# A four-mixer decoder layer on one core: the mixers' rank against the dense products, and finer tracing

## The chip, the core and the metric

The kernel runs on one core of a Trainium2 chip. The metric is the device time of one execution in microseconds.

## What is computed

One layer of a hybrid recurrent decoder, for 512 prompt positions and 8 sequences of 8 sample positions (576 columns in all), in float32. The input is normalised, one projection feeds four token mixers (ssd: Mamba-2; s5: a diagonal state space; hg: HGRN2; rw: RWKV-7), their outputs are gated, merged and projected back, and a gated MLP with a short convolution follows. Cut to the core:

```python
proj = rmsnorm(x, norm1_w) @ w_in
y_ssd, y_s5, y_hg, y_rw = ssd_mixer(...), s5_mixer(...), hgrn_mixer(...), rwkv_mixer(...)
gates = sigmoid(xn @ w_merge + b_merge)
merged = (gates[0] * (y_ssd @ w_br_ssd) + gates[1] * (y_s5 @ w_br_s5)
          + gates[2] * (y_hg @ w_br_hg) + gates[3] * (y_rw @ w_br_rw))
x = x + merged @ w_out
up = causal_dwconv(rmsnorm(x, norm2_w) @ ffn_up)
x = x + (gelu(up_gate) * up_val) @ ffn_down
```

The mixers' new states are outputs too.

## The kernel before

**Dense products.** Activations lie transposed, 128 features by 576 columns, each split into a high and a low part. A weight tile is loaded by SP (`weights`, L182), cast to its high part on ACT (L169) and subtracted to its low part on DVE or POOL (L170). `dense` (L211) makes an output tile of 128 x 576 in two halves of 288 columns; `part` (L219) issues three products per 128 inputs: high by high (L223), high by low (L224), low by high (L225), names `dn`. A dense tile of eight inputs is thus 48 products. The evacuation of a half and all of a weight tile's instructions have rank HIGH.

**Mixers.** Each is a generator that issues a piece of its work and yields a number, the piece's cost. Their products are small, their results are named `mxrw`, `mxs`, `mxhg` and `mxssd`. rw runs as stream "a", s5, hg and ssd one behind the other as stream "b". The last steps of rw (from L1795) write the sample states out: products (L1797), transposes (L94), a copy on ACT (L1806) into one buffer, tB, and two stores; then `finish` normalises each of two heads' groups in two column pieces (L1835 to L1849): head sums on PE (L1423, L1424), a square (L1838), a reciprocal root on DVE (L176 to L180), three steps on POOL up to L1848. These use tB too.

**Order of the work.** The order on the engines has two stages. First `drive` (L2288) traces three streams: "a", "b" and `dense_stream` (L2199). It always continues the stream with the lowest clock, and adds to that clock what the generator yields; for a mixer, times a factor of SLOW (L29). Then a scheduler lays the traced instructions out on each engine: of those that it holds ready it takes the one of lowest rank. An instruction's rank is its number in the trace less an offset, and a mixer's offset is HIGH, a million: a ready mixer instruction goes ahead of every dense product. On the chip each engine then takes its instructions in that order.

**Dense stream.** `dense_stream` traces the projections u, rw, hg, dt, xbc and z (55 tiles). Then it computes gate tiles ahead (`gate`, L427) and stores them to memory (`spill`), up to 32, as long as the mixers are not done. When stream "a" is done ("a" in `done`), the pools `late`, `gp` and `yp` are opened in the place of rw's, the S5 outputs are loaded (yg, L446; `load_split`) and turned into the GLU's input yh, and there follow the GLU (L2181), the branches rw, s5, hg, ssd (`branch`, L473) and the tail: w_out and the MLP. A gate that was not stored is computed within its branch.

Of the kernel before, what the change touches and what calls it, by code (L numbers as in the profile page):

```python
# [25 lines left out]
GELU = 0.7978845608028654  # L26
HIGH = 1000000

SLOW = {"rw": 4.65, "s5": 1.62, "hg": 2.88, "ssd": 1.86}  # L29


STRASSEN = (1, 0, 1, 0, 0, 0, 1, 0, 0, 0, 1)
# [8 lines left out]
class Kern:  # L41
# [169 lines left out]
    def dense(self, w, k0, kt, c0, mt, xh, xl, evac, inner=None):  # L211

        for m in range(mt):
            wt = self.weights(w, k0, kt, c0 + m * P, inner)
            for j in range(2):
                self.part(wt, slice(j * H2, (j + 1) * H2), xh, xl, m, evac)
            yield m

    def part(self, wt, sl, xh, xl, m, evac):  # L219
        nc = self.nc  # L220
# [181 lines left out]
def project(K, name, c0, order):  # L402

    nc, tc = K.nc, K.tc
    for m in order:
        st = K.stage.tile([P, T], F32, tag="st", name=K.n("st"))

        def evac(_, sl, ps, st=st):
            if name == "u":

                nc.scalar.copy(out=st.rearrange("p (s c) -> p s c", s=LS)[:, :, sl.start // LS:sl.stop // LS],
                               in_=ps.rearrange("p (c s) -> p s c", s=LS))
            else:
                nc.scalar.copy(out=st[:, sl], in_=ps)

        for _ in K.dense(K.I["w_in"][0], 0, 8, c0 + m * P, 1, K.xh, K.xl, evac, 16 if name == "u" else None):
            d = K.dram.tile([LS, P, T // LS] if name == "u" else [P, T], F32, name=f"pd_{name}{m}")
            with tc.high_priority(offset=HIGH):
                if name == "u":
                    nc.sync.dma_start(out=d.rearrange("s p c -> p s c"), in_=st.rearrange("p (s c) -> p s c", s=LS))  # L420
                else:
                    nc.sync.dma_start(out=d, in_=st)
            K.proj[(name, m)] = d
            yield 6000


def gate(K, b, m, g):  # L427

    nc = K.nc

    def evac(_, sl, ps):
        nc.scalar.activation(g[:, sl], ps, AF.Tanh, bias=K.vc("b_merge", b * 8 + m), scale=0.5)  # L432

    for _ in K.dense(K.I["w_merge"][0], 0, 8, b * D + m * P, 1, K.xh, K.xl, evac):
        yield 6000


def load_split(K, y, scale=None, turn=False, keep=None):
# [34 lines left out]
def branch(K, b, wname, ys, cols=None, done=None):  # L473

    nc, tc = K.nc, K.tc
    yh, yl = [h for h, _ in ys], [l for _, l in ys]
    kt = len(ys)
    for m in range(8):
        g = K.gp.tile([P, T], F32, tag="g", name=K.n("g"))
        if (b, m) in K.gates:  # L480
            nc.sync.dma_start(out=g, in_=K.gates[(b, m)])
        else:
            yield from gate(K, b, m, g)
        first = not K.started[m]
        K.started[m] = True

        def evac(_, sl, ps):
            o = K.merged[m] if first else g
            nc.vector.scalar_tensor_tensor(out=o[:, sl], in0=g[:, sl], scalar=1.0, in1=ps, op0=ALU.add, op1=ALU.mult)  # L489

        for _ in K.dense(K.I[wname][0], 0, kt, m * P, 1, yh, yl, evac):
            if cols is not None:
                nc.gpsimd.tensor_tensor(out=g, in0=g, in1=cols, op=ALU.mult)
            if not first:
                nc.gpsimd.tensor_tensor(out=K.merged[m], in0=K.merged[m], in1=g, op=ALU.add)
            if done:
                done(m)
            yield 750 * kt


def conv_state_out(K, cs, ktaps, nt, prompt, sample, pool):
# [65 lines left out]
def tail(K):  # L567
# [27 lines left out]
    with K.mc:  # L595
# [48 lines left out]
            nc.vector.tensor_tensor(out=x1[m][:, sl], in0=ps, in1=res[m][:, sl], op=ALU.add)  # L644

        for m in K.dense(I["w_out"][0], 0, 8, 0, 8, mh, ml, evac):
            with tc.high_priority(offset=HIGH):
                sides(m)
            if m == 0:
                nc.scalar.activation(acc, x1[m], AF.Square)  # L650
            else:
                sq = K.stage.tile([P, T], F32, tag="st", name=K.n("sq"))
                nc.scalar.activation(sq, x1[m], AF.Square)
                (nc.vector if m == 7 else nc.gpsimd).tensor_tensor(out=acc, in0=acc, in1=sq, op=ALU.add)
# [106 lines left out]

    K.spare["t"] += ["c", "w", "w"]
    for m in K.dense(down, k0, n, 0, LAST, ah, al, evac):
        if m:
            turn(m - 1)
        if m == 1:
            states_out()
# [54 lines left out]
def hgrn(K, ctx):  # L822
# [41 lines left out]
    def head(h):  # L864
# [108 lines left out]
        for c in range(4):  # L973
            cs = slice(c * P, (c + 1) * P)
            nc.tensor.matmul(po[:, cs], vt[:, c, :], att[:, cs], start=True, stop=c == 0)
            if c:
                nc.tensor.matmul(po[:, cs], S[:, c - 1, :], qR[:, cs], start=False, stop=True)
        nc.scalar.copy(out=o[:, :TP], in_=po)
        pso = K.ps()
        S0 = wk("S0", (P, NS, P), 1)  # L980
        nc.sync.dma_start(out=S0, in_=I["state_hgrn"][0, :, h].rearrange("b k v -> k b v"))
        nc.tensor.matmul(pso[:, :64], svt, satt, start=True, stop=False)
        for b in range(NS):
            nc.tensor.matmul(pso[:, b * LS:(b + 1) * LS], S0[:, b, :], qR[:, TP + b * LS:TP + (b + 1) * LS],
                             start=False, stop=b == NS - 1)
        nc.scalar.copy(out=o[:, TP:], in_=pso[:, :64])
        yield 3500
        nc.gpsimd.tensor_tensor(out=S0, in0=S0, in1=stot[:, 64:72].unsqueeze(2).to_broadcast([P, NS, P]), op=ALU.mult)
        for j in range(2):
            bs = slice(j * 4, j * 4 + 4)  # L990
            vm = wk("kt", (P, 4, P))[:64]
            nc.gpsimd.tensor_tensor(out=vm, in0=svt.unsqueeze(1).to_broadcast([64, 4, P]),
                                    in1=sm[:64, bs].unsqueeze(2).to_broadcast([64, 4, P]), op=ALU.mult)
            pt = K.ps()
            nc.tensor.matmul(pt, skt, vm.rearrange("p b v -> p (b v)"), start=True, stop=True)
            sv = S0[:, bs, :].rearrange("p b v -> p (b v)")
            nc.vector.tensor_tensor(out=sv, in0=sv, in1=pt, op=ALU.add)
        nc.sync.dma_start(out=O["s_hgrn"][0, :, h].rearrange("b k v -> k b v"), in_=S0)
        yield 3000

        sq, rn = f, kL
        nc.scalar.activation(sq, o, AF.Square)
# [53 lines left out]
def s5(K, ctx):  # L1056
# [142 lines left out]
    for qt in range(4):  # L1199
# [41 lines left out]
        for a in range(GP):  # L1241
            for ri, cb in ((0, cbr), (1, cbi)):
                nc.tensor.matmul(pk[:, a * 32:(a + 1) * 32], W[ri][:, a].rearrange("p s j -> p (s j)"), cb[:, a, :],
                                 start=ri == 0, stop=ri == 1)
        yield 4000

        Kc = wp.tile([P, 8, 16], F32, tag="Kc", name=K.n("Kc"))
        TT(out=Kc, in0=pk[:, :P].rearrange("p (g j) -> p g j", j=16), in1=dsk[:, qt * 8:(qt + 1) * 8, :], op=ALU.add)
# [13 lines left out]
        for ri in range(2):  # L1262
# [3 lines left out]
                    es = slice(g2 * 64, g2 * 64 + 64)  # L1266
                    nc.tensor.matmul(pt[es, b * NCK:(b + 1) * NCK], Mz[:, b, ri, es], U[:, 2 * b + g2, :], start=True, stop=True)
            nc.scalar.copy(out=Z[:, ri].rearrange("p g c -> p (g c)"), in_=pt[:, :GP * NCK])
        yield 2500

        E = Z[:, :, :, :NPC].rearrange("p r g (c k) -> p r g c k", k=8)
        a8r, a8i = Pr[:, 8, gs], Pi[:, 8, gs]
# [40 lines left out]
        for g2 in range(2):  # L1313
            es = slice(g2 * 64, g2 * 64 + 64)
            pt = K.ps()
            for a in range(GP):
                gq = 2 * a + g2
                o = pt[:, a * NCK:(a + 1) * NCK]
                nc.tensor.matmul(o, Mt[:, gq].rearrange("p t j -> p (t j)"), U[:, gq, :], start=True, stop=False)
                for ri in range(2):  # L1320
                    nc.tensor.matmul(o, Mc[ri][es, a].rearrange("p t j -> p (t j)"), H[es, ri, a, :], start=False, stop=ri == 1)
            nc.scalar.copy(out=Y.rearrange("p (a g) c -> p g a c", g=2)[:, g2], in_=pt[:, :4 * NCK].rearrange("p (a c) -> p a c", a=GP))
            yield 2000
        d = K.dram.tile([P, T], F32, name=f"y_s5{qt}")
        dv = d.rearrange("(g j) (t c) -> t j g c", j=16, c=NCK)
        for t in range(8):
# [529 lines left out]
def ssd(K, ctx):  # L1856
# [135 lines left out]
    for hf in range(2):  # L1992
# [10 lines left out]
        for c in (4, 0, 1, 2, 3):  # L2003
# [74 lines left out]
            if samp:  # L2078
# [6 lines left out]
                for q in range(2):  # L2085
# [6 lines left out]
                    for b in range(0, NS, 4):  # L2092
                        pt = K.ps()
                        for b2 in range(4):
                            K.turn(pt[:, b2 * P:(b2 + 1) * P], h0[:, b + b2].rearrange("p g n -> p (g n)"))
                        nc.scalar.copy(out=h0T[b // 4], in_=pt.rearrange("p (b q) -> p b q", b=4))
                    po = K.ps()[:, :P]
                    for b in range(NS):
                        nc.tensor.matmul(po[:, b * 16:(b + 1) * 16], h0T[b // 4][:, b % 4, :], CS[:, b].rearrange("p g t -> p (g t)"), start=True, stop=True)
                    od = wk("Gm", (P, P), 2)  # L2100
                    TT(out=od.rearrange("p (g b t) -> p g b t", g=2, t=LS), in0=po.rearrange("p (b g t) -> p g b t", g=2, t=LS),
                       in1=eB.rearrange("p (g q) (b t) -> p q g b t", g=2, t=LS)[:, q], op=ALU.mult)
# [3 lines left out]
                    for g in range(2):  # L2106
# [3 lines left out]
                                         start=True, stop=True)  # L2110
                        TT(out=h0[:, :, g, :], in0=h0[:, :, g, :], in1=pn.rearrange("p (b n) -> p b n", b=NS), op=ALU.add)
                        nc.sync.dma_start(out=view(O["s_ssd"][0], g), in_=h0[:, :, g, :])
                    yield 3500
            elif c:
                po = K.ps()
                for q in range(2):
# [64 lines left out]
def glu(K, ys, yt):  # L2181
# [3 lines left out]
    for m in range(4):  # L2185
# [3 lines left out]
            nc.scalar.activation(g[:, sl], ps, AF.Tanh, bias=K.vc("s5_glu_b", m), scale=0.5)  # L2189

        for _ in K.dense(K.I["s5_glu_w"][0], 0, 4, m * P, 1, yh, yl, evac):
            nc.vector.scalar_tensor_tensor(out=g, in0=g, scalar=1.0, in1=yt[:, m], op0=ALU.add, op1=ALU.mult)
            d = K.dram.tile([P, T], F32, name=f"y_s5g{m}")
            nc.sync.dma_start(out=d, in_=g)
            K.y_s5g.append(d)
            yield 3000


def dense_stream(K):  # L2199
# [88 lines left out]
def drive(K, streams):  # L2288

    live = [[0, i, g, nm] for i, (g, nm) in enumerate(streams)]  # L2290
    while live:
        s = min(live, key=lambda v: v[:2])
        try:
            if s[3]:
                K.stream, K.label = s[3], K.now.get(s[3], "")
                with K.tc.high_priority(offset=HIGH):
                    s[0] += SLOW[K.now.get(s[3], "rw")] * max(next(s[2]), 1)
            else:
                s[0] += max(next(s[2]), 1)
# [47 lines left out]
```

## Time and profile before

| | us |
|---|---|
| median of 3 runs | 1699.29 |
| runs | 1692.22, 1699.29, 1717.2 |
| the profiled execution | 1718.78 |
| its span, first to last instruction | 1717.1 |
| PE busy in the span | 1629.7 |
| DVE, POOL, ACT busy | 1186.2, 789.6, 696.0 |

The profile is one execution. PE is the engine of matrix products, DVE, ACT and POOL work elementwise, SP issues the DMAs. A busy time is the union of the shown durations of an engine's instructions; products overlap, so the distance from start to start says more than a duration. The granted clock has two levels, 1.0 (2.4 GHz) and 0.5 (1.2 GHz); a value between is a mean over a stretch.

### The profile page before, as it was taken

How to read it: one execution, taken by the hardware profiler on the slowest of the kernel's cores; microseconds unless marked ns; L12 is line 12 of the kernel's file. 1: busy time of each engine (PE TensorE's matmuls, PEld its weight loads, DVE VectorE, ACT ScalarE, POOL GpSimd, SP SyncE). 2: the span in 40 equal slices, each digit the busy share in tenths (PEclk: the TensorE clock that was granted, in tenths of full speed). 3: DMA queues.
4: the chain of work that ended last, by engine and by line, in shares of the span. 5: the costliest groups of instructions: out<-in, count | busy, mean ns of one | idle time of the engine just before them, and what ended most of it. 6: DMA issues, size and time to landing. Idle time of an engine off the chain costs nothing. (4 is left out here: it accounts for less than half of the span.)

```text
span 1717.1 us, 32744 instructions
## 1 busy us (share of the span) xinstructions
PE 1629.7 (95%) x12164; PEld 1473.1 (86%) x12164; DVE 1186.2 (69%) x2584; ACT 696.0 (41%) x1489; POOL 789.6 (46%) x1013
## 2 busy tenths in 40 slices
PE   6989999999999999999998999998998999999997
PEld 4888888888798898778887988888998999989897
DVE  7888886986684388333347664695479975985985
ACT  6333232433343344222245353332356643653653
POOL 5645342534322464121244563375676734743750
PEclk7999888998899999879999999999999999999999
DMA  7555553642462455231345553665422332232332
GB/s 202 141 129 138 139 119 84 174 120 77 142 182 75 122 168 163 63 99 59 100 145 155 152 161 100 203 193 156 124 90 75 99 99 74 75 99 74 87 105 71
DMA packets 356453, 207.62 MB, mean 121 GB/s; under 512 B 110884, under 2 KB 328358, under 8 KB 356294
## 3 DMA queue, kind: packets, MB, share of 16 engines
q1 hardware_dynamic: 356293, 205.53, 42.6%
q8 instruction: 96, 1.57, 0.4%
q14 instruction: 64, 0.52, 0.1%
HBM read 151.54 MB, written 53.02 MB: 119 GB/s over the span
## 5 line engine op out<-in xcount | busy, mean ns | idle before, releaser
L223 PE MATMUL dn<-xh,whi 128*128 128x288 f32 x1392 | 430.1, 309 | 6.4 <-ACT gst L432 2.7
L224 PE MATMUL dn<-xl,whi 128*128 128x288 f32 x1392 | 431.8, 310 | 1.9 <-DVE xl L170 1.6
L225 PE MATMUL dn<-xh,wlo 128*128 128x288 f32 x1392 | 428.5, 308 | 0.0
L223 PEld LDWEIGHTS dn<-xh,whi 128*128 128x128 f32 x1392 | 271.4, 195 | 22.4 <-issue 9.1
L224 PEld LDWEIGHTS dn<-xl,whi 128*128 128x128 f32 x1392 | 271.8, 195 | 15.8 <-issue 8.5
L225 PEld LDWEIGHTS dn<-xh,wlo 128*128 128x128 f32 x1392 | 271.6, 195 | 10.7 <-issue 7.0
L169 ACT CAST whi<-wraw 128x512 fp32r<-128x512 f32 (+1 forms) x278 | 173.4, 628 | 236.4 <-PE dn L224 225.9
L170 POOL TENSOR_TENSOR wlo<-wraw,whi 128x512 fp32r<-128x512 f32 x92 | 131.4, 1429 | 195.2 <-ACT whi L169 171.1
L170 DVE TENSOR_TENSOR wlo<-wraw,whi 128x512 fp32r<-128x512 f32 (+1 forms) x186 | 150.5, 810 | 81.2 <-ACT whi L169 68.5
L262 PE MATMUL dn<-big,whi 128*128 128x288 f32 x528 | 108.6, 298 | 8.6 <-ACT su L286 3.0
L247 POOL TENSOR_TENSOR wlo<-wraw,whi 128x512 fp32r<-128x512 f32 x66 | 89.6, 1365 | 48.3 <-ACT whi L246 48.1
L223 PE MATMUL dn<-yh,whi 128*128 128x288 f32 x352 | 105.9, 304 | 4.9 <-DVE g L489 2.8
L262 PE MATMUL dn<-xh,whi 128*128 128x288 f32 x352 | 104.8, 299 | 4.7 <-ACT whi L246 4.2
L224 PE MATMUL dn<-yl,whi 128*128 128x288 f32 x352 | 105.9, 301 | 2.1 <-DVE yl L167 2.0
L262 PE MATMUL dn<-xh,wlo 128*128 128x288 f32 x352 | 103.6, 298 | 4.4 <-POOL wlo L247 4.4
L225 PE MATMUL dn<-yh,wlo 128*128 128x288 f32 x352 | 106.4, 304 | 0.0
L262 PE MATMUL dn<-xl,whi 128*128 128x288 f32 x352 | 103.5, 295 | 0.0
L223 PE MATMUL dn<-ah,whi 128*128 128x288 f32 (+2 forms) x324 | 95.1, 298 | 1.5 <-ACT ah L169 1.5
L224 PE MATMUL dn<-al,whi 128*128 128x288 f32 (+2 forms) x324 | 95.5, 296 | 0.6 <-DVE al L170 0.6
L225 PE MATMUL dn<-ah,wlo 128*128 128x288 f32 (+2 forms) x324 | 95.0, 295 | 0.0
L262 PEld LDWEIGHTS dn<-big,whi 128*128 128x128 f32 x528 | 84.3, 188 | 12.4 <-ACT su L286 4.5
L262 PE MATMUL dn<-big,wlo 128*128 128x288 f32 x264 | 77.7, 295 | 0.1
(741 smaller groups left out, 4094.4 us busy)
## 6 DMA issues: line engine op xcount, KB each, us to landing
wraw<-w_in SPq DMA_DIRECT2D x55, 512.0 KB
wraw<-ffn_up SPq DMA_DIRECT2D x44, 512.0 KB
wraw<-w_merge SPq DMA_DIRECT2D x32, 512.0 KB
gate<-gst SPq DMA_DIRECT2D x32, 288.0 KB
g<-gate SPq DMA_DIRECT2D x32, 288.0 KB
wraw<-ffn_down SPq DMA_DIRECT2D x16, 448.0 KB
pd_hg<-st SPq DMA_DIRECT2D x16, 288.0 KB
wraw<-w_br_ssd SPq DMA_DIRECT2D x8, 512.0 KB
```

The lines of the kernel that those rows point to most:

```text
L169: nc.scalar.copy(out=hi, in_=src)
L170: lo_engine.tensor_tensor(out=lo, in0=src, in1=hi.bitcast(F32), op=ALU.subtract)
L223: nc.tensor.matmul(ps, wh, xh[k][:, sl], start=k == 0, stop=False)
L224: nc.tensor.matmul(ps, wh, xl[k][:, sl], start=False, stop=False)
L225: nc.tensor.matmul(ps, wl, xh[k][:, sl], start=False, stop=k == len(wt) - 1)
L247: TT[eng](out=lo, in0=src, in1=hi.bitcast(F32), op=ALU.subtract)
L262: nc.tensor.matmul(ps, wt[:, k], x, start=start and k == 0 and i == 0, stop=k == n - 1 and i == 2, skip_group_check=not start)
```

## The change

The offset of the mixers falls from HIGH to AHEAD = 50: a mixer instruction ranks 50 numbers ahead of what is traced beside it, and no longer ahead of all dense work. The SLOW factors are multiplied by 0.35. `dense` yields after each half of a tile, with half the cost, and its users pass that on. hg, s5 and ssd yield in smaller pieces, whose costs add up to about the old ones. Weights and evacuations keep HIGH. What is computed stays the same. The diff, cut to its kinds (the other added yields in hg, s5, ssd and the GLU are of the same kind):

```diff
-SLOW = {"rw": 4.65, "s5": 1.62, "hg": 2.88, "ssd": 1.86}
+SLOW = {"rw": 4.65 * 0.35, "s5": 1.62 * 0.35, "hg": 2.88 * 0.35, "ssd": 1.86 * 0.35}
+
+AHEAD = 50
...
             for j in range(2):
                 self.part(wt, slice(j * H2, (j + 1) * H2), xh, xl, m, evac)
-            yield m
+                yield m if j else None
...
         for _ in K.dense(K.I["w_in"][0], 0, 8, c0 + m * P, 1, K.xh, K.xl, evac, 16 if name == "u" else None):
+            if _ is None:
+                yield 3000
+                continue
...
-            yield 6000
+            yield 3000
...
         for _ in K.dense(K.I[wname][0], 0, kt, m * P, 1, yh, yl, evac):
+            if _ is None:
+                yield 375 * kt
+                continue
...
-            yield 750 * kt
+            yield 375 * kt
...
         nc.scalar.copy(out=o[:, :TP], in_=po)
+        yield 900
...
             nc.vector.tensor_tensor(out=sv, in0=sv, in1=pt, op=ALU.add)
+            yield 1000
...
-        yield 4000
+            if a % 2:
+                yield 2000
...
                         nc.scalar.copy(out=h0T[b // 4], in_=pt.rearrange("p (b q) -> p b q", b=4))
+                        yield 500
...
-                    yield 3500
+                        yield 850
...
-                with K.tc.high_priority(offset=HIGH):
+                with K.tc.high_priority(offset=AHEAD):
                     s[0] += SLOW[K.now.get(s[3], "rw")] * max(next(s[2]), 1)
```

How the order on PE changes is shown at three places. The first is in S5, in the first half of the projections; `W` are tiles that are transposed for the next quarter. Before:

```order
L94 MATMUL mxs_656_4527<-ident,W_4389 128x128
L94 MATMUL mxs_656_4527<-ident,W_4390 128x128
L1651 MATMUL mxrw_4961<-Q_721_4954,bk_4956 128x128
L1769 MATMUL mxrw_4937<-UV_3953,BT_3961 64x64
L1651 MATMUL mxrw_4962<-Q_722_4955,bk_4956 128x128
L1651 MATMUL mxrw_4961<-Q_721_4954,bk_4956 128x128
L1651 MATMUL mxrw_4962<-Q_722_4955,bk_4956 128x128
L1546 MATMUL mxrw_5224<-rwwa,wup_1603 128x256
L225 MATMUL dn_2604<-xh_107,wlo_2597 128x288
```

The same kind of place after the change (lines are up to 25 higher):

```order
L96 MATMUL mxs_396_2624<-ident,W_2571 128x128
L96 MATMUL mxs_396_2624<-ident,W_2572 128x128
L1711 MATMUL mxrw_3282<-L_518_3280,NT_1484 64x64 x2
L1711 MATMUL mxrw_3282<-L_518_3280,NT_1485 64x64 x2
L1563 MATMUL mxrw_3748<-rwwa,wup_1490 128x256
L227 MATMUL dn_3704<-xh_109,wlo_3701 128x288
L225 MATMUL dn_3704<-xh_110,whi_3700 128x288
L226 MATMUL dn_3704<-xl_118,whi_3700 128x288
```

Before, this run has 37 small products with no dense one between them, the outputs of the last quarter ahead of the rows shown; after the change it has 13, and 16 dense products follow.

The second place is the end of rw on PE, before the change; `rwshn` is the shift state, rw's last two products, and `dn_8777` a gate:

```order
L225 MATMUL dn_8777<-xh_105,wlo_8744 128x288
L94 MATMUL mxrw_12785<-ident,rwshn 14x128
L223 MATMUL dn_8777<-xh_106,whi_8743 128x288
L224 MATMUL dn_8777<-xl_114,whi_8743 128x288
L225 MATMUL dn_8777<-xh_106,wlo_8744 128x288
L223 MATMUL dn_8777<-xh_107,whi_8743 128x288
L2099 MATMUL mxssd_11643<-sscs_9845,Rl_11629 128x16 x4
L2099 MATMUL mxssd_11643<-sscs_9845,xd_11630 128x16 x4
L2109 MATMUL mxssd_11656<-Rh_11584,xe_11483 128x512
L94 MATMUL mxrw_12790<-ident,rwshn 112x128
L224 MATMUL dn_8777<-xl_115,whi_8743 128x288
```

They stand among the products of a gate. The third is the same end after the change, in two pieces; `dn_12237` is the last gate that is stored, `tB` rw's sample state:

```order
L225 MATMUL dn_12237<-xh_111,whi_12207 128x288
L226 MATMUL dn_12237<-xl_119,whi_12207 128x288
L227 MATMUL dn_12237<-xh_111,wlo_12208 128x288
L96 MATMUL mxrw_11712<-ident,tB_11538 64x128 x4
L2092 MATMUL mxssd_10196<-M_10176,xd_10033 64x128 x2
L2139 MATMUL mxssd_10229<-sscb_7092,hT_9547 128x256 x2
L2092 MATMUL mxssd_10196<-M_10176,xd_10033 64x128 x2
```

From the fourth of these rows on no dense product stands in the queue for 88 products, until the end of rw and the first product of the GLU on `yh`:

```order
L1443 MATMUL mxrw_12154<-hs_12150,rwbones 128x256
L1444 MATMUL mxrw_12154<-hs_12151,rwbones 128x256
L96 MATMUL mxrw_12263<-ident,rwshn 14x128
L96 MATMUL mxrw_12268<-ident,rwshn 112x128
L225 MATMUL dn_12370<-yh_12323,whi_12366 128x288
L225 MATMUL dn_12384<-yh_12323,whi_12366 128x288
L225 MATMUL dn_12408<-yh_12323,whi_12404 128x288
```

So rw's state writes and last normalisations, and the last chunks of ssd, which stood between dense products, now stand together. 24 gates are stored ahead instead of 32; the other eight are computed within the ssd branch.

## Rows read from the trace of the kernel before

**Rows 1.** The page: busy us, share and count by engine; granted clock by slice.

```profile
PE 1629.7 (95%) x12164; PEld 1473.1 (86%) x12164; DVE 1186.2 (69%) x2584; ACT 696.0 (41%) x1489; POOL 789.6 (46%) x1013
...
PEclk7999888998899999879999999999999999999999
```

**Rows 2.** Timeline of PE at 731 and 751 us: start, duration, instruction.

```profile
731.30 0.29 PE L223 MATMUL dn<-xh,whi 128*128 128x288 f32 x1
731.43 0.29 PE L224 MATMUL dn<-xl,whi 128*128 128x288 f32 x1
...
751.64 0.44 PE L224 MATMUL dn<-xl,whi 128*128 128x288 f32 x1
751.88 0.44 PE L225 MATMUL dn<-xh,wlo 128*128 128x288 f32 x1
```

**Rows 3.** Stretches: length, busy (count) by engine, granted clock, DMA share, GB/s.

```profile
22.00:988.00 966.00, 932.46 (x7174) 807.67 (x7174) 644.62 (x1686) 344.57 (x811) 393.36 (x622) 0.93 0.46 126
988.00:1232.00 244.00, 230.03 (x1593) 212.37 (x1592) 148.75 (x204) 85.12 (x147) 128.04 (x87) 0.98 0.53 158
1232.00:1717.10 485.10, 456.19 (x3354) 445.36 (x3353) 381.32 (x675) 251.44 (x507) 262.21 (x288) 1.00 0.30 87
```

**Rows 4.** The same for PE's products of line 225 alone.

```profile
22.00:988.00 966.00, 390.10 (x1263) 0.93 0.46 126
```

**Rows 5.** The same for ssd's products on PE alone.

```profile
22.00:988.00 966.00, 69.85 (x330) 0.93 0.46 126
988.00:1232.00 244.00, 31.85 (x152) 0.98 0.53 158
```

**Rows 6.** PE in an idle stretch and in the eleven of low clock before 988.

```profile
125.50:128.90 3.40, 0.00 (x0) 1.00 1.06 291
128.90:135.70 6.80, 6.00 (x40) 0.53 0.26 69
187.00:193.80 6.80, 6.74 (x29) 0.52 0.51 141
248.40:272.30 23.90, 23.90 (x142) 0.51 0.25 45
...
750.20:780.90 30.70, 30.70 (x142) 0.50 0.29 73
sum 119.30, PE 118.45; mean PE 10.77
```

**Rows 7.** Timeline of ACT and POOL, 884 to 1018: the end of rw, yg.

```profile
884.62 0.58 ACT L1806 COPY tB<-mxrw 64x512 f32<-64x512 f32 x1 [1.06 <-POOL X L2122]
894.01 0.58 ACT L1806 COPY tB<-mxrw 64x512 f32<-64x512 f32 x1 [0.63 <-DMA s_rwkv<-tB]
922.41 0.57 ACT L1806 COPY tB<-mxrw 64x512 f32<-64x512 f32 x1
927.78 0.58 ACT L1806 COPY tB<-mxrw 64x512 f32<-64x512 f32 x1 [3.15 <-DMA s_rwkv<-tB]
934.92 0.47 ACT L1838 ACTIVATE tB<-Y 128x320 f32<-128x320 f32 x1
946.97 0.42 ACT L1838 ACTIVATE tB<-Y 128x256 f32<-128x256 f32 x1 [2.93 <-POOL Y L1845]
958.31 0.47 ACT L1838 ACTIVATE tB<-Y 128x320 f32<-128x320 f32 x1
975.11 0.41 ACT L1838 ACTIVATE tB<-Y 128x256 f32<-128x256 f32 x1
...
987.91 1.26 POOL L1848 TENSOR_TENSOR Y<-Y,tA 128x256 f32<-128x256 f32 x1
...
998.26 0.69 ACT L448 ACTIVATE yst<-yg 128x576 f32<-128x576 f32 x1 [4.28 <-DMA yg<-y_s]
1005.28 0.67 ACT L166 ACTIVATE yh<-yg 128x576 fp32r<-128x576 f32 x1
...
1017.17 0.69 ACT L166 ACTIVATE yh<-yg 128x576 fp32r<-128x576 f32 x1
```

More of the change, by code (lines that the diff above doesn't have):

```diff
@@ L434, in gate @@
     for _ in K.dense(K.I["w_merge"][0], 0, 8, b * D + m * P, 1, K.xh, K.xl, evac):
-        yield 6000
+        yield 3000
 def load_split(K, y, scale=None, turn=False, keep=None):
@@ L646, in tail @@
         for m in K.dense(I["w_out"][0], 0, 8, 0, 8, mh, ml, evac):
+            if m is None:
+                continue
             with tc.high_priority(offset=HIGH):
@@ L763, in tail @@
     for m in K.dense(down, k0, n, 0, LAST, ah, al, evac):
+        if m is None:
+            continue
         if m:
@@ L977, in head @@
                 nc.tensor.matmul(po[:, cs], S[:, c - 1, :], qR[:, cs], start=False, stop=True)
+            if c == 1:
+                yield 700
         nc.scalar.copy(out=o[:, :TP], in_=po)
+        yield 900
         pso = K.ps()
@@ L985, in head @@
                              start=False, stop=b == NS - 1)
+            if b == 3:
+                yield 900
         nc.scalar.copy(out=o[:, TP:], in_=pso[:, :64])
-        yield 3500
+        yield 1000
         nc.gpsimd.tensor_tensor(out=S0, in0=S0, in1=stot[:, 64:72].unsqueeze(2).to_broadcast([P, NS, P]), op=ALU.mult)
@@ L997, in head @@
             nc.vector.tensor_tensor(out=sv, in0=sv, in1=pt, op=ALU.add)
+            yield 1000
         nc.sync.dma_start(out=O["s_hgrn"][0, :, h].rearrange("b k v -> k b v"), in_=S0)
-        yield 3000
+        yield 1000
         sq, rn = f, kL
@@ L1268, in s5 @@
             nc.scalar.copy(out=Z[:, ri].rearrange("p g c -> p (g c)"), in_=pt[:, :GP * NCK])
-        yield 2500
+            yield 1250
         E = Z[:, :, :, :NPC].rearrange("p r g (c k) -> p r g c k", k=8)
@@ L1321, in s5 @@
                     nc.tensor.matmul(o, Mc[ri][es, a].rearrange("p t j -> p (t j)"), H[es, ri, a, :], start=False, stop=ri == 1)
+                yield 450
             nc.scalar.copy(out=Y.rearrange("p (a g) c -> p g a c", g=2)[:, g2], in_=pt[:, :4 * NCK].rearrange("p (a c) -> p a c", a=GP))
-            yield 2000
+            yield 200
         d = K.dram.tile([P, T], F32, name=f"y_s5{qt}")
@@ L2099, in ssd @@
                         nc.tensor.matmul(po[:, b * 16:(b + 1) * 16], h0T[b // 4][:, b % 4, :], CS[:, b].rearrange("p g t -> p (g t)"), start=True, stop=True)
+                    yield 800
                     od = wk("Gm", (P, P), 2)
@@ L2112, in ssd @@
                         nc.sync.dma_start(out=view(O["s_ssd"][0], g), in_=h0[:, :, g, :])
-                    yield 3500
+                        yield 850
             elif c:
@@ L2191, in glu @@
         for _ in K.dense(K.I["s5_glu_w"][0], 0, 4, m * P, 1, yh, yl, evac):
+            if _ is None:
+                yield 1500
+                continue
             nc.vector.scalar_tensor_tensor(out=g, in0=g, scalar=1.0, in1=yt[:, m], op0=ALU.add, op1=ALU.mult)
@@ L2195, in glu @@
             K.y_s5g.append(d)
-            yield 3000
+            yield 1500
 def dense_stream(K):
```

## The prediction

> **What bounds the kernel now.** I read the page's first two parts, then busy time and clock by stage, then the timeline, and last the chains at the end of the mixers. The page says PE 95% busy, at a clock below 1 in a dozen of its slices [rows 1]. That is not PE at its peak: at full clock the dense products start 0.131 us apart though each is shown as 0.29 us long [rows 2]. The stages [rows 3] say more. The stretch 22 to 988 us holds all mixer work of rw, s5 and hg and most of ssd, and 3,792 of the 8,394 dense products (counted in the order of the PE queue; line 225 holds one in three, and its 1,263 records in this stretch agree [rows 4]). At 0.133 us these need 504 us; the other 460 us go to the mixers' small products, to 33.5 us in which no product is shown running (966 less 932.5), and to the clock, whose mean there is 0.93. From 988 to 1232 us run 1,440 dense products (191 us) and the last 152 products of ssd [rows 5], and from 1232 us the tail, whose PE order the change leaves as it is.
>
> The clock is worth reading closely. In eleven stretches before 988 us, 119 us in all, the granted clock is 0.5, that is 1.2 GHz ([rows 6] hold four of the eleven, and the sum), and dense products start 0.24 us apart there [rows 2]. Just ahead of most of these stretches PE runs small products and few dense ones; ahead of 128.9 us it ran nothing at all [rows 6]. As products run there at about half pace, the 119 us cost about 60.
>
> **The change part by part.** Before, a mixer instruction that is ready goes ahead of every dense product, so ready mixer work stands in runs. Ranked 50 ahead, with dense work traced in halves and the mixers in pieces, it is mixed more finely: between the first dense product and the 3,792nd, the PE order has 24 runs of more than 16 small products (626 in them) before and 17 (421 in them) after. If the low clock goes with the products in long runs, it keeps 421/626 = 0.67 of its cost and gives back 0.33 x 60 = 20 us. Bounds: 0 (the runs that are left may fall as badly) and 60 (all of it goes).
>
> Of the 33.5 us of idle PE I take back 5. A mixer product that comes later in PE's queue finds its input ready more often, but the number of PE rows between a rw product and the last instruction that feeds it is 20 in the median against 18, so little changes. Bounds: -10 (mixers delayed, their successors waited for) and 33.5.
>
> On ACT, DVE and POOL the weight splits and evacuations keep their old rank and now stand ahead of mixer work; on SP weight loads pass the mixers' loads and stores. I cost this at nothing before 988 us: PE has dense products to run while a mixer waits. That cover is what ends next.
>
> The mixers' factors of 0.35 let them be traced further ahead, and "a" is done after 24 gates in trace order instead of after all 32 (the stores of gates on SP count 32 before, 24 after). So no dense work is left to trace until the inputs of the GLU, the S5 output and the other branches are there, and these lie in pools that open only when the rw mixer's pools have closed. In the order of before, the last rw product stands between dense products. In that of after, 88 small products follow the 3,792nd dense product with no dense one between them: rw's sample state writes, its last four normalisations, and two and a half chunks of ssd. PE takes products in order, so every later dense product waits for this chain, and behind it for the first input of the GLU.
>
> How long is this hole? The same chain stands in the trace, ready work first [rows 7]:
> - From the end of the first state copy (885.2) to the first square of the normalisations (934.9): 50 us. It holds two copies that wait for DMA stores and a POOL wait on the same; its own operations are some 8 us and four store waits some 5 each (922.98 to 927.78 is 4.8), so 28 is the floor.
> - Four normalisations, from 934.9 to the end of POOL's last addition (987.91 + 1.26 = 989.2): 54 us, in rounds of 12.1, 11.3, 16.8 and 14.1. Floor: 4 x 11.3 = 45.
> - From there to the first square of yg (998.3, it waited for the load) and to the first yh (1005.3): 16 us; floor 14. The fourth yh is cast only at 1017.2, which may hold the first GLU products 5 us more.
> At the pace of before that is 125 us, at its floor 87. Before, the chain shared DVE, ACT and POOL with weight splits, evacuations and the convolutions of ssd, and its PE steps queued behind dense products; after the change the splits and evacuations are mostly absent, but two and a half ssd chunks run beside it. I take 105, nearer to the middle than to either end.
>
> Before, PE covered this time with the last eight gates (384 products, 51 us) and ssd's last work. The eight gates are not saved: they are now computed within the ssd branch. Only the small products in the hole are work that had to be done anyway: they are mainly the set that follows 988 us before, 152 for 31.9 us [rows 5]. I take 30. So the hole adds 105 - 30 = 75 us; bounds 87 - 32 = 55 and, if ssd and rw slow each other, 135 - 30 = 105.
>
> PE is nearly idle in the hole. Where it ran nothing (125.5 to 128.9) the next 6.8 us had clock 0.53 [rows 6], a loss of about 3 us; I add 3 once, for the products behind the hole. The Trainium skill, "TensorE: Matmul & The Clock Gate", section "Why this matters for your kernels", warns that idle stretches between bursts send PE back to half clock; the trace agrees at this place. By that rule the hole's own small products would also run at 1.2 GHz throughout; an estimate from it is 30 us more of PE time, of which perhaps a third lies on the rw chain: 10 us instead of 3, and the sum 1759.
>
> Sum on the profiled execution: 1718.8 + 75 - 20 - 5 + 3 = 1772. That execution lies at the top of the three runs (1692 to 1717, median 1699.3), so the difference of +53 goes on the median: **1752 us**.
>
> **The rivals.**
> 1. The clock repays the hole: the finer mix keeps PE at 2.4 GHz from 187 to 781 us. For it: 119 us at low clock, 60 us of price, and PE's idle 33.5. Against it: seventeen long runs are left, one of 38 products. It decides from the point at which clock and idle give back more than the hole adds: with 60 + 15 against 75 + 3 the time is 1702. With 48 us given back it is +30, still within 2%.
> 2. The change wins outright: all of 60 + 33.5 come back and the hole is at its floor of 55 net, + 3: 1699 - 36 = 1663. It needs every favourable end at once, or a gain in 22 to 988 us beyond the clock that I don't see.
> 3. The hole is longer. The ssd chunks share DVE and POOL with the normalisations, both with rank 50, and the clock stays at 1.2 GHz through it: 105 net + 10, less 15 of gain: 1799.
> 4. The change doesn't do what it says: early runs are as they were, no gain, and the hole is covered because the chain finishes early. PE's in-order queue and the pools that open late speak against the second half. About 1700.
>
> **How the numbers follow.** Forecast (hole of 55 to 100 net, gain of 10 to 40): 0.58, own range 1725 to 1785. Rivals 1 and 4 together 0.22, rival 2 0.11, rival 3 0.09. About 2% is what a measurement of this kernel can tell from no change: 1665 and 1733. Of the forecast 0.05 falls within 2%; rivals 1 and 4 lie there, rival 3 is slower, rival 2 faster (one in five of it within 2%). Faster 0.09, same 0.29, slower 0.62. The range that should hold 8 in 10 reaches down to rival 1's case: 1695 to 1792.
>
> **What would show it.** In the profile after: two or more slices around 1000 us where PE is busy for less than half, with the clock well below 1 behind them, and PE's waits named by rw's normalisations, by ssd or by the load of yg; from the first yh product on, 1,440 dense products until w_out's first in about 215 us instead of 244; before the hole a mean clock above 0.93, and the 3,792nd dense product some 20 us earlier than 988 us. The tail should take 485 us as before. The forecast is wrong if PE stays over 80% busy at that place, or if the dense products before it end more than 60 us earlier.

## The result, and the profile after the change

The changed kernel takes 1764.62 us (median of 4 runs, 1761.79 to 1775.63), the kernel before beside it 1700.65 us (4 runs, 1692.22 to 1717.2): a ratio of 1.0384, 95% interval 1.0335 to 1.0434, 64 us slower. The forecast was 1752, in a range of 1695 to 1792. The profiled execution took 1763.09 us, its span 1761.3. The profiled execution before (1718.78 us) was a slow one, 1.6% above the fastest in the table, so its stages are set beside two later executions of the same order too.

The page of the changed kernel: busy times, and PE's busy share and granted clock by slice; the last row is PE's busy share before.

```profile
PE 1640.1 (93%) x12164; PEld 1470.6 (83%) x12164; DVE 1176.6 (67%) x2584; ACT 697.8 (40%) x1489; POOL 785.0 (45%) x1013
...
PE   6989999999999999999999945999999999999998
...
PEclk7999989989899999999999957999999999999999
...
PE   6989999999999999999998999998998999999997
```

Two slices, the 24th and 25th, have PE at 4 and 5 tenths and the clock at 5 and 7; before, PE is at 8 tenths or more in every slice but the first and the last. By stretches of the changed kernel (columns as in [rows 3]; the last row is the part of low clock):

```profile
22.00:994.50 972.50, 943.52 (x7193) 807.02 (x7193) 634.81 (x1672) 338.73 (x798) 386.76 (x608) 0.95 0.46 124
994.50:1074.60 80.10, 33.96 (x136) 17.42 (x134) 50.32 (x82) 21.72 (x43) 44.06 (x44) 0.63 0.23 70
1074.60:1275.70 201.10, 194.79 (x1438) 192.78 (x1439) 98.99 (x137) 70.38 (x118) 87.25 (x59) 0.99 0.50 148
1275.70:1761.30 485.60, 456.06 (x3353) 445.26 (x3351) 380.62 (x675) 251.56 (x507) 261.77 (x288) 0.99 0.30 87
...
1018.90:1080.00 61.10, 19.97 (x54) 11.65 (x55) 39.59 (x58) 18.84 (x37) 32.79 (x33) 0.50 0.18 57
```

The hole, the stretch in which PE has next to no dense product, is there: 80.1 us with 34 us of products. Before and behind it stand two other differences. The 3,792 dense products ahead of it end at about 995 us where they ended at 988 [rows 3], later, not earlier. And from the first product on yh to w_out it takes 201 us, where the same 1,440 dense products with ssd's rest took 244 [rows 3]. The tail is as it was, 485.6 us. PE's waits in the changed kernel from 994 to 1082 us (total, times, longest):

```profile
PE dn L225 <- ACT yh L168: 16.6, 2, 16.2
PE mxrw L1443 <- ACT hs L171: 12.8, 3, 6.4
PE mxssd L2092 <- DVE M L2084: 5.8, 3, 2.3
PE mxssd L2198 <- POOL ssacc L2193: 4.0, 1, 4.0
```

They carry the names of the prediction: the GLU's input, rw's normalisations (hs are the split operands of their head sums), ssd's chunks. The chain itself, ACT's timeline (POOL's last addition of the fourth normalisation ends at 1063.4):

```profile
992.05 0.58 ACT L1826 COPY tB<-mxrw 64x512 f32<-64x512 f32 x1 [0.60 <-PE mxrw L96]
...
1011.60 0.58 ACT L1826 COPY tB<-mxrw 64x512 f32<-64x512 f32 x1 [3.58 <-PE mxrw L96]
1016.44 0.58 ACT L1826 COPY tB<-mxrw 64x512 f32<-64x512 f32 x1 [1.20 <-DMA s_rwkv<-tB]
1019.87 0.47 ACT L1858 ACTIVATE tB<-Y 128x320 f32<-128x320 f32 x1 [0.70 <-DMA s_rwkv<-tB]
...
1042.41 0.47 ACT L1858 ACTIVATE tB<-Y 128x320 f32<-128x320 f32 x1 [2.96 <-POOL Y L1865]
...
1068.07 0.68 ACT L453 ACTIVATE yst<-yg 128x576 f32<-128x576 f32 x1 [1.65 <-DMA yg<-y_s]
...
1074.11 0.67 ACT L168 ACTIVATE yh<-yg 128x576 fp32r<-128x576 f32 x1
```

From the first state copy's end to the first square 27.2 us, four normalisations 43.5, then 10.7 to the first yh: 81 us.

### The profile page after: what moved, and what is told of

The parts are those of the page before. It is cut to its first block, busy times and chain, and to the rows that moved or that the text cites. A ratio compares the mean times of both kernels' runs of the same rounds, so it can differ in the third digit from the quotient of the medians.

```text
span 1761.3 us, 32717 instructions
## 1 busy us (share of the span) xinstructions
PE 1640.1 (93%) x12164; PEld 1470.6 (83%) x12164; DVE 1176.6 (67%) x2584; ACT 697.8 (40%) x1489; POOL 785.0 (45%) x1013
## 5 line engine op out<-in xcount | busy, mean ns | idle before, releaser
L227 PE MATMUL dn<-xh,wlo 128*128 128x288 f32 x1392 | 435.3, 313 | 0.0
L172 POOL TENSOR_TENSOR wlo<-wraw,whi 128x512 fp32r<-128x512 f32 x92 | 127.6, 1387 | 262.9 <-ACT whi L171 259.5
L225 PE MATMUL dn<-yh,whi 128*128 128x288 f32 x352 | 101.4, 299 | 22.1 <-ACT yh L168 17.5
L249 POOL TENSOR_TENSOR wlo<-wraw,whi 128x512 fp32r<-128x512 f32 x66 | 89.8, 1368 | 48.1 <-ACT whi L248 48.0
L264 PE MATMUL dn<-xh,wlo 128*128 128x288 f32 x352 | 103.6, 298 | 4.4 <-POOL wlo L249 4.4
L225 PEld LDWEIGHTS dn<-yh,whi 128*128 128x128 f32 x352 | 65.4, 190 | 23.9 <-POOL yst L455 16.5
```

The lines of the kernel that those rows point to most:

```text
L172: lo_engine.tensor_tensor(out=lo, in0=src, in1=hi.bitcast(F32), op=ALU.subtract)
L225: nc.tensor.matmul(ps, wh, xh[k][:, sl], start=k == 0, stop=False)
L227: nc.tensor.matmul(ps, wl, xh[k][:, sl], start=False, stop=k == len(wt) - 1)
L249: TT[eng](out=lo, in0=src, in1=hi.bitcast(F32), op=ALU.subtract)
L264: nc.tensor.matmul(ps, wt[:, k], x, start=start and k == 0 and i == 0, stop=k == n - 1 and i == 2, skip_group_check=not start)
```

## The experiments

Ratios are to the kernel before, run beside each group, with 95% intervals. "Front" is the stretch from 22 us to the 3,792nd dense product; each row's boundary is where that product, or its neighbour, runs.

**The hole covered.** All 32 gates are stored before the GLU:

```diff
-        if now and (now[0] != "ssd" or len(steps) == 1):
+        if now and not spill and (now[0] != "ssd" or len(steps) == 1):
```

> The changed kernel with all 32 gates traced and stored before the GLU may begin. Rank 50, factors of 0.35 and the finer tracing stay; in the PE order the 88 small products without a dense one between them are gone (38 is then the longest such run). Theory T1, the loss is the hole: it is 80.1 us long in the changed kernel, of which its own small products (mxssd x96, mxrw x32) take 35, so some 45 us go, a few more with the cold products behind it: 1705 to 1725 us, no stretch with PE under half busy near 1000 us, and the first product on yh later than the 4,000th dense product. Theory T2, the low rank costs everywhere because the mixers' products come later: nothing is repaid, 1750 to 1770 us. Theory T3, the factors and the finer tracing cost by themselves: the same as T2, 1750 to 1770.

1739.92 us, ratio 1.0223 [1.0181, 1.0264], between the ranges of T1 and T2. Some 25 us of the 64 are repaid, not 45. Stretches of this run:

```profile
22.00:996.90 974.90, 944.77 (x7204) 808.45 (x7204) 634.83 (x1673) 340.18 (x799) 387.51 (x609) 0.95 0.46 125
996.90:1066.00 69.10, 69.10 (x485) 60.77 (x482) 38.37 (x64) 25.77 (x52) 34.33 (x34) 1.00 0.39 119
1066.00:1105.00 39.00, 14.39 (x64) 11.19 (x62) 29.63 (x35) 16.42 (x30) 23.60 (x19) 0.61 0.30 90
```

The place of the old hole is full (69.1 of 69.1 us busy), but the gates end before rw's chain does and a hole of 39 us is left behind them (PE's longest wait in it, 12.6 us, is for ssd's last sum, the next for yh). And the front is as long as in the changed kernel, 974.9 us. So neither T1 nor T2 is enough alone.

**The rank alone undone.** In the changed kernel `high_priority(offset=AHEAD)` becomes `offset=HIGH`.

> The changed kernel with the mixers' offset set back to a million; factors of 0.35 and finer tracing stay, 24 gates are stored ahead. The PE order has no hole, since rw's last products stand ahead of dense ones (last rw product at the 3,577th dense product). T1 (the hole): 1685 to 1715 us, as the kernel before. T2 (the low rank everywhere): also 1685 to 1715. T3 (factors and finer tracing cost by themselves): 1740 to 1770.

1689.87 us, ratio 0.9930 [0.9894, 0.9967]: the finer tracing and the factors together cost nothing, T3 falls, and the whole loss hangs on the rank. There is no hole: from 986.9 to 1203.9 us PE is busy 211.4 of 217 us.

**The factors alone.** The kernel before with the four factors times 0.35.

> The kernel before with the four factors multiplied by 0.35 and nothing else. 24 gates are stored ahead of the GLU instead of 32, and there is no hole in the PE order (last rw product at the 3,680th dense product, first product on yh at the 3,784th). T1 and T2: 1685 to 1715 us, as before. T3: 1740 us or more. If 24 gates alone were too few, PE would stand idle ahead of the first product on yh, for at most the 16 us that the changed kernel waits there: 1715.

1679.95 us, ratio 0.9866 [0.9826, 0.9906]: faster than the kernel before. 24 stored gates are enough where rw ends in time. It is also 10 us faster than the run above, which has the finer tracing besides: the finer tracing gains nothing here, and seems to cost some of what the factors gain.

**The rank alone done.** The kernel before with `offset=50` in place of HIGH.

> The kernel before with the offset of 50 and nothing else: factors and tracing as they were. Since the mixers are then traced late, all 32 gates are traced while much of rw and all that follows is not, and 1,063 small products stand in the PE order without a dense one between them, behind the 4,176th. T1 (a hole costs what its chain takes, less its own products): the 88 products of the changed kernel took 80 us, 35 of them products; 1,063 products at the same 0.5 us of net loss each are some 540 us, with bounds of 200 and 800: 1900 to 2500 us. T2 (a loss by rank spread over the kernel, no more of it where the hole is longer): 1750 to 1800. T3 (factors and tracing): 1685 to 1715.

1942.19 us, ratio 1.1399 [1.1345, 1.1453], as T1 has it and near the low end of its bounds. The hole of this run:

```profile
908.00:1311.40 403.40, 311.23 (x1933) 199.30 (x1933) 259.26 (x547) 118.74 (x282) 181.73 (x264) 0.60 0.28 75
```

403 us with next to no dense work, at a mean clock of 0.60. With the factors as they were, the low rank leaves half of the mixers' work for the time after the last gate. It is the factors of 0.35, with the finer tracing, that kept the changed kernel's hole at 80 us.

**Which stream makes the hole.** The changed kernel with the old rank for one stream only:

```diff
-                with K.tc.high_priority(offset=AHEAD):
+                with K.tc.high_priority(offset=HIGH if s[3] == "a" else AHEAD):
```

> The changed kernel with the offset of a million for rw alone (stream a); s5, hg and ssd stay at 50. rw's last product stands at the 3,434th dense product, and no long run of small products ahead of the first product on yh; 111 products of ssd now stand together behind the 4,608th dense product, ahead of the ssd branch. Theory A, rw comes late because its instructions wait behind dense work at rank 50, and so ends after the dense work that could cover it: the hole at 995 us is gone and rw's last product ends before 960 us; what is lost is a smaller hole ahead of the ssd branch, 111 products at the 0.3 to 0.7 us each that products in holes took so far, 33 to 78 us, 28 of them work: 1695 to 1740 us. Theory B, the ssd chunks in the hole set its length: 1740 us or more, with the wait ahead of the ssd branch as long as the 80 us of the changed kernel.

1748.30 us, ratio 1.0236 [1.0169, 1.0303]. Its stretches, with the hole in the last row but one:

```profile
22.00:958.30 936.30, 898.38 (x7096) 789.45 (x7097) 660.71 (x1680) 347.45 (x819) 403.42 (x627) 0.93 0.48 132
958.30:1075.00 116.70, 113.22 (x847) 110.16 (x845) 57.77 (x92) 36.46 (x63) 50.94 (x35) 1.00 0.60 181
1075.00:1187.00 112.00, 67.76 (x248) 40.54 (x248) 46.82 (x79) 20.18 (x36) 27.08 (x26) 0.56 0.16 40
1187.00:1264.20 77.20, 77.15 (x582) 76.91 (x581) 27.24 (x42) 24.28 (x42) 32.90 (x23) 1.00 0.33 94
```

As theory A said, the hole at 995 us is gone with rw's lateness (rw's last product ends at 899 us). But ssd, now the late one, makes a hole of its own ahead of its branch, and at 112 us a longer one than I had allowed for: its products ran at half clock through nearly all of it. The time lies outside A's range and in B's.

The reverse, `offset=AHEAD if s[3] == "a" else HIGH`:

> The reverse: a million for s5, hg and ssd (stream b), 50 for rw. 76 small products still stand together behind the 3,792nd dense product. Theory A (rw's own chain is the hole): PE stays under half busy for 65 to 85 us there, and 1740 to 1770 us. Theory B (ssd's chunks set its length): the hole falls below 50 us and the time to 1700 to 1725.

1773.06 us, ratio 1.0385 [1.0315, 1.0456], 3 us above A's range; the hole lasts 78.9 us, as in the changed kernel and as A has it:

```profile
22.00:999.00 977.00, 952.19 (x7201) 805.50 (x7202) 641.96 (x1677) 342.22 (x799) 385.44 (x611) 0.95 0.45 123
999.00:1077.90 78.90, 33.60 (x129) 17.52 (x129) 47.81 (x78) 22.67 (x45) 43.85 (x42) 0.63 0.24 70
```

With ssd at its old rank nothing is gained: at the changed kernel's 995 us it is rw's chain that counts.

**The price of a change between dense and small products.** The kernel before, with small products that add zero put into the tail's `part`, in one run per half tile, or each alone:

```diff
             nc.tensor.matmul(ps, wl, xh[k][:, sl], start=False, stop=k == len(wt) - 1)
+            for _ in range((len(wt) - 1) if self.zero is not None and k == len(wt) // 2 - 1 else 0):
+                nc.tensor.matmul(ps[:64, :64], self.zero[:64], self.ident[:64, :64], start=False, stop=False)
```

(`self.zero` is a tile of zeros made at the start of the tail; for the products alone the range is `1 if self.zero is not None and k < len(wt) - 1 else 0`. Each of the 416 shows as two records, x2.)

> A measurement of the price of a change between dense and small products, on the kernel before, in the tail where the clock is 1.0 and no mixer runs. Into the dense products of w_out and of the first part of down, 416 small products are put (64x64 weights, 64 columns, weights zero, adding nothing to the sums), seven or so in one run in the middle of each half tile, some 60 runs. Theory S (a change from dense to small and back costs time of its own): from the distances in the trace of before (dense to small 0.224 us, small to small 0.045, small to dense 0.149, dense to dense 0.133) a run of seven costs 0.224 + 0.149 - 0.133 + 6 x 0.045 = 0.51 us, 416 of them 30 us. Theory N (no such price): 416 x 0.045 to 0.1, 19 to 42 us. The next run tells them apart.

> The same 416 small products, but each alone between dense products. Theory S: 0.224 + 0.149 - 0.133 = 0.24 us each, 100 us in all, 70 us more than with the runs of seven. Theory N: the same as with the runs, within 10 us. If S holds, the 130 more changes of the changed kernel ahead of its 3,780th dense product cost some 20 us, what the clock gave back there.

In runs 1767.90 us, ratio 1.0354 [1.0266, 1.0442], 55 us more than before; alone 1950.72 us, ratio 1.1426 [1.1352, 1.1500], 238 us more. The same products cost four times as much where each stands alone, so N falls; S has the direction right and both sizes, 30 and 100 us, too small. In the profiled executions the tail alone grows from 485.1 us to 555.7 and 741.2, by 71 and 256. Some of that is the clock. PE's timeline with a run of seven:

```profile
1240.44 0.29 PE L226 MATMUL dn<-mh,wlo 128*128 128x288 f32 x1
1240.66 1.02 PE L228 MATMUL dn<-ident,zero 64*64 64x64 f32 x14
1241.62 0.40 PE L224 MATMUL dn<-mh,whi 128*128 128x288 f32 x1
1241.86 0.29 PE L225 MATMUL dn<-ml,whi 128*128 128x288 f32 x1
1241.99 0.29 PE L226 MATMUL dn<-mh,wlo 128*128 128x288 f32 x1
```

and with single ones, at full clock:

```profile
1513.63 0.33 PE L228 MATMUL dn<-ident,zero 64*64 64x64 f32 x2
1513.88 0.40 PE L224 MATMUL dn<-ah,whi 128*128 128x288 f32 x1
1514.12 0.30 PE L225 MATMUL dn<-al,whi 128*128 128x288 f32 x1
1514.25 0.29 PE L226 MATMUL dn<-ah,wlo 128*128 128x288 f32 x1
1514.47 0.32 PE L228 MATMUL dn<-ident,zero 64*64 64x64 f32 x2
```

From one single product to the next is 0.84 us, with three dense products that take 3 x 0.131 = 0.39 by themselves [rows 2]: a single one costs 0.45 us. A run of seven takes 1.55 us from 1240.44 to 1241.99, less three dense ones 1.16, or 0.12 for each product beyond the first. So a change to this kind of small product and back costs about 0.33 us by itself, twice what I had put down; it includes the second dense product behind the change, which starts 0.24 us after the first and not 0.13. The rest of the single products' cost is the clock's, and stands in the last section.

The price belongs to the kind of product, which neither run varied. In the changed kernel a transposition of 128 rows between two dense products has none:

```profile
952.29 0.30 PE L225 MATMUL dn<-xh,whi 128*128 128x288 f32 x1
952.43 0.27 PE L96 MATMUL mxssd<-ident,B 128*128 128x128 f32 x1
952.46 0.38 PE L226 MATMUL dn<-xl,whi 128*128 128x288 f32 x1
952.67 0.29 PE L227 MATMUL dn<-xh,wlo 128*128 128x288 f32 x1
```

From 952.29 to 952.67 it adds 0.11 us to two dense distances, and in the same trace two such in a row add 0.22, four 0.44 and eight 0.88: each its own time and nothing for the change. rw's head sums (L1443, L1444) add 0.14 alone and 0.30 as a pair. Four transpositions of 64 rows add 0.59. Why the kinds differ stays open.

The two runs with added products also give the front of the kernel before, untouched, two more times:

```profile
22.00:964.00 942.00, 908.99 (x7177) 789.59 (x7178) 648.00 (x1689) 345.54 (x815) 402.95 (x625) 0.97 0.47 130
```

for the runs of seven, and for the single ones

```profile
22.00:973.00 951.00, 917.17 (x7177) 796.21 (x7178) 646.10 (x1689) 345.23 (x814) 401.57 (x624) 0.95 0.47 128
```

With [rows 3] the same front took 966, 942 and 951 us in three executions, at mean clocks of 0.93, 0.97 and 0.95: the low clock of [rows 6] is not a fixed property of the order. The changed kernel's front has clock 0.95 too, as many products, and takes 972.5 us, 21.5 more than the third of these, with 26 us more of busy PE. The clock records of the three traces hold 135, 61 and 98 us at 1.2 GHz in this stretch, the changed kernel's 106. From the first to the second execution 74 us less of it saved 23.5 us of busy time, about a third and not a half.

**Between the two ranks.** The changed kernel with `AHEAD = 400`, and with `AHEAD = 1000`:

> The changed kernel with the offset 400 instead of 50. Two things are set apart: the PE order has 366 changes from dense to small products ahead of the 3,780th dense product (291 before, 421 after the change), and 64 small products still stand behind the 3,792nd without a dense one between, nearly all of rw; ssd's last chunks are no longer among them. Theory: a change from dense to small and back costs 0.15 to 0.18 us and rw's chain alone sets the hole. Then the 3,780th dense product comes some 10 us earlier than in the changed kernel (993), the hole is still 60 to 80 us long with only 10 to 20 us of products in it, and the time is 1745 to 1770 us. Rival: the ssd products in the hole were what made it long; then it is under 50 us and the time 1720 or less.

> The changed kernel with the offset 1000: 297 changes, no long run of small products at the end of rw (its last product at the 3,637th dense product). Theory (changes and hole are all that the low rank costs): 1685 to 1705 us, as with an offset of a million. Rival (any offset below the dense work's rank costs, through weight splits that go ahead of mixers on ACT, DVE and POOL): 1715 us or more.

400 gives 1725.60 us, ratio 1.0114 [1.0064, 1.0164]; 1000 gives 1690.81, ratio 0.9925 [0.9898, 0.9952], as with a million. My expectation for 400 fell between its two cases and had the names the wrong way round; its 3,780th dense product comes some 6 us earlier than in the changed kernel, not 10. The rival for 1000 falls. The hole of the run with 400, all of PE and then ssd's products alone:

```profile
988.90:1034.90 46.00, 29.34 (x109) 15.34 (x108) 31.14 (x53) 10.95 (x24) 28.15 (x30) 0.60 0.27 82
...
988.90:1034.90 46.00, 26.36 (x97) 0.60 0.27 82
```

It is filled by ssd, not emptied of it, and yet it is shorter, because rw's chain had got further. ACT's timeline of this run:

```profile
988.53 0.47 ACT L1858 ACTIVATE tB<-Y 128x320 f32<-128x320 f32 x1 [0.62 <-POOL Y L1865]
...
1034.26 0.67 ACT L168 ACTIVATE yh<-yg 128x576 fp32r<-128x576 f32 x1
```

The third normalisation begins as the dense work ends; in the changed kernel most of the state writes were then still to come. The hole is what is left of rw's chain when the dense work ends. That rest runs slower here, 45.7 us from the third square to the first yh against 31.7 (1042.41 to 1074.11); the products of ssd's chunks run beside it until 1032 us, and in the changed kernel they end at 1028, ahead of its third square, so they are the likely cause.

These runs also set the front's length beside the number of changes from dense to small products ahead of the 3,780th dense product. First offset 400, then 1000, then the million (the rank alone undone):

```profile
22.00:988.90 966.90, 935.62 (x7218) 804.62 (x7219) 656.70 (x1690) 343.46 (x811) 413.42 (x618) 0.95 0.46 126
22.00:978.50 956.50, 917.66 (x7220) 795.81 (x7221) 666.07 (x1708) 350.42 (x827) 426.29 (x636) 0.95 0.47 130
22.00:986.90 964.90, 919.44 (x7234) 796.80 (x7234) 678.80 (x1720) 355.57 (x836) 424.71 (x641) 0.95 0.47 130
```

All fronts with a mean clock of 0.95, with the changes counted in the traces:

| order | changes | front, us | PE busy, us |
|---|---|---|---|
| before (single products' run) | 291 | 951 | 917.2 |
| offset 1000 | 297 | 956.5 | 917.7 |
| offset a million | 302 | 964.9 | 919.4 |
| offset 400 | 366 | 966.9 | 935.6 |
| changed kernel | 421 | 972.5 | 943.5 |
| 32 gates | 421 | 974.9 | 944.8 |
| 50 for rw alone | 435 | 977 | 952.2 |

Busy time rises with the count, by 0.20 to 0.25 us for each change from the first row to each of the last four. The count isn't all: the factors alone have 324 changes and less busy time (895.1 us in their second run, shown below) than the order of before at the same mean clock of 0.97 (909.0).

**A version that beats both.** The kernel before with factors times 0.4, and again with 0.35:

> The kernel before with the factors times 0.4: 32 gates are stored as before (first product on yh at the 4,133rd dense product), 291 changes, ssd's last product at the 4,470th dense product (4,656th before, 4,337th with 0.35). If the gain of the factors alone (1.3% with 0.35) comes from mixers that are traced earlier, half or more of it stays: 1683 to 1697 us. If it comes from the eight gates that are not stored and read back, it is gone: 1698 to 1708.

> The kernel before with the factors times 0.35 and nothing else, once more and in five rounds, as the version that may beat both: 1672 to 1690 us, ratio 0.980 to 0.993. If the first measurement was the scatter between executions, 0.995 or more.

0.4: 1699.51 us, ratio 0.9953 [0.9918, 0.9987]. 0.35: 1675.71 us, ratio 0.9823 [0.9783, 0.9863], the second measurement of this kernel and like the first; it is 32 us faster than the kernel before and some 90 faster than the changed one. Its stretches:

```profile
22.00:962.60 940.60, 895.12 (x7252) 777.69 (x7253) 670.08 (x1718) 353.80 (x829) 428.95 (x639) 0.97 0.48 132
962.60:1184.60 222.00, 211.84 (x1518) 202.38 (x1517) 123.35 (x175) 77.30 (x132) 104.78 (x72) 0.98 0.49 143
```

The gain stands in the second: 222 us where [rows 3] have 244, with 75 products fewer in it. These were done in the front, which is no longer for it. With 0.4 less than half of the gain is left, as the case of the eight gates' stores has it; but ssd's end moves with the factor too, so what the gain is made of stays open.

## Why the prediction was right, and where it was not

- **The hole and its cause: right.** 88 products without dense ones, PE below half there, waits by rw, ssd and the GLU's input. Undoing the rank alone (1689.87) or setting the offset to 1000 (1690.81) removes it and the whole loss; the two runs with one stream at its old rank show that in the changed kernel it is rw's lateness.
- **Its size: too large.** I took 105 us from [rows 7], "nearer to the middle than to either end" of 87 and 125; it is 80.1, below the floor. Part by part: 27.2 where I had 50 and a floor of 28, 43.5 where I had 54 and 45, 10.7 where I had 16 and 14. I had allowed too little for what slowed the chain before, the work that shared its engines or the dense products ahead of its steps on PE; no run tells these apart. The products in it are 34 us where I took 30. From the front's end to w_out the changed kernel takes 80.1 + 201.1 = 281.2 us, before 244 [rows 3] and, in the two later executions, 243.1 and 238.2: +37 to +43, not +75. Behind the hole, 201 us instead of the 215 I forecast: PE has 6.3 us without a product there, before 14.
- **The front: wrong, the step that failed.** I had it 25 us shorter, 20 by the clock ("it keeps 421/626 = 0.67 of its cost and gives back 0.33 x 60 = 20 us") and 5 by idle time. The idle time came as forecast: PE has 29.0 us without a product (972.5 less 943.5), before 33.5. The clock gain did not. Its base, 119 us at low clock [rows 6], belonged to that one execution: the same order had 135, 61 and 98 us of it in the whole front, the changed one 106, so no gain stands out from the scatter, and each such us cost about a third and not a half. That the mean clock before the hole is above 0.93, a sign I had named, therefore shows nothing. And the front is longer: 972.5 us against 942 and 951 in the two later executions of the order before, +26, or +19.5 against the mean of all three. What I left out is the price of a change between dense and small products, 421 of them ahead of the 3,780th dense product instead of 291 (80 and 72 of these lead to transpositions of 128 rows or head sums alone, which had no such price). At the 0.15 us that the distances in the trace of before give (0.224 + 0.149 - 0.133, less about 0.09 for the product itself) to the 0.33 of the single products, 130 more cost 20 to 43 us. The order with the rank at 50 for rw alone, with 435 changes, is as long (977); with rw high and the others at 50 it has 294 and takes 936, with fewer of ssd's products. That these changes are the cause rests on the count, which the fronts at equal clock follow, and on the measured price; no run altered the count and nothing else.
- **The clock in the hole: nearer to the page than to my row.** I added 3 us. From 1018.9 to 1080 us the clock is 0.50, so the hole's last 56 us and the first dense products ran at 1.2 GHz. The Trainium skill, "TensorE: Matmul & The Clock Gate", section "Why this matters for your kernels", warns that idle stretches between bursts send PE back to half clock. The trace agrees in part: PE's waits of 16.2, 6.4, 6.0 and 4.0 us all lie in the stretch at 0.50, but the clock had fallen ahead of them, at 1018.9, when PE had waited 2.3 us at most between the hole's small products.
- **The sum.** I had +78 for the hole and what lies behind it and -25 for the front, +53. Measured: +40.5 and +26 against the two later executions, 66.5, and +39 and +19.5 against all three, 59; the medians differ by 64. The total came out near because two errors, 38 us too much for the hole and 51 too little for the front (39 and 44 against all three), cancelled, which is luck. Rival 1, the clock that repays, and rivals 2 and 4 are out. Rival 3 had the half clock right and the length wrong. The tail was as predicted.

## What to carry to other kernels

A low rank for a chain of dependent work costs no wait while independent work is left to run beside it, and all of the chain's rest once that is used up: compare where the chain ends with where its cover ends, on the engine that takes work in order, before lowering a rank. Mixing small products finely among dense ones can have a price per change on PE, by the kind of product, so count the changes and not only the long runs. And take a quantity like the time at low clock from several executions before building a gain on it.

## What the runs showed of the hardware

A change from dense products (128 x 128 weights, 288 columns) to a small one (64 x 64, 64 columns) and back took about 0.33 us beyond the small product's own share in a run, at full clock, as worked out above; transpositions of 128 rows between dense products took 0.11 us each and nothing for the change.

The clock can stay low under a PE that is never shown idle. In the run of single products PE waited 2.67 us for the tile of zeros, at the start of w_out; then:

```profile
1215.90:1386.00 170.10, 170.10 (x611) 126.36 (x611) 39.07 (x55) 29.10 (x56) 33.48 (x30) 0.50 0.10 30
1490.00:1600.00 110.00, 109.12 (x676) 84.60 (x675) 29.80 (x51) 18.86 (x34) 16.04 (x16) 1.00 0.15 44
```

For 170 us, with one single product after every three dense ones, PE was busy throughout and the clock stayed at 1.2 GHz; later the same pattern, come to at full clock, kept 2.4 GHz. A group of three dense products and a single one took 1.42 us in the first stretch and 0.84 in the second, against 0.39 without the single one. So some 120 of the 416 cost 1.03 us each and the rest 0.45, about 255 us together; the tail of this run is 256 us longer than before. In the run with sevens, which had no such wait, the clock was 1.00 through this part of the tail. What keeps the clock down there was not tried.
